# Mixer C's six projection tiles moved from the first stage to the low-priority dense work beside mixer A's recurrence

## The chip, the cores and the metric

The kernel runs on one core of one Trainium2 chip. The metric is the device time of one execution in microseconds (us); lower is better. Beside the time of each run there is one profiled execution, with every engine's instructions: PE (TensorE, matmuls; PEld its weight loads), DVE (VectorE), ACT (ScalarE), POOL (GpSimd) and SP, whose queue issues most of the DMAs.

## The reference

One layer of a hybrid decoder trunk, in float32, for 2048 prompt tokens and 8 x 8 sample tokens (2112 tokens in all) of width 1024. One combined projection `x @ w_in` feeds three mixers; their outputs are projected, normalised, and pass a gated feed-forward block. Cut to what matters here:

```python
proj = x @ w_in
(qa, ka, va, za, ba, aa, xb, gb, qc, kc, vc, zc, lc) = jnp.split(proj, SPLIT_POINTS, axis=-1)

# mixer A: gated DeltaNet, 6 heads of 64, causal conv on q, k, v, chunks of 64 tokens
qkv, dconv_new = causal_dwconv(jnp.concatenate([qa, ka, va], axis=-1), st_dconv, conv_a_w)
qa, ka, va = jnp.split(jax.nn.silu(qkv), [QK_A, 2 * QK_A], axis=-1)
...
oa, delta_new = gated_delta_chunked(l2norm(qa) * DK_A ** -0.5, l2norm(ka), va, beta, g, st_delta)
oa = head_rms_norm(oa, norm_a_w) * jax.nn.silu(za)

# mixer B: RG-LRU of width 256 on xb, gated by gelu(gb)
...
# mixer C: gated linear attention, 6 heads (dk=32, dv=64); q and k are 192 wide, v and z 384
qc = qc * DK_C ** -0.5
logf = jax.nn.log_sigmoid((lc @ gla_w2 + gla_b2)) / GLA_TAU
oc, gla_new = gla_chunked(qc, kc, vc, logf, st_gla)
oc = head_rms_norm(oc, norm_c_w) * jax.nn.silu(zc)

heads = jnp.concatenate([oa, ob, oc], axis=-1)
x = layer_norm(ALPHA * x + heads @ w_out, ln1_g, ln1_b)
f, fconv_new = conv_ffn(x, st_fconv, ffn_w_up, ffn_conv_w, ffn_conv_b, ffn_w_down)
x = layer_norm(ALPHA * x + f, ln2_g, ln2_b)
```

## The kernel before

A float32 product is made from three single-pass matmuls over operands that are split into two rounded parts, high and low: `wh*xh`, `wl*xh` and `wh*xl`. A rounded part `h` is an ACT copy, the rest `lo` is a subtraction on DVE or POOL. Projections are cut into tiles of 128 columns of `w_in` and blocks of tokens; a tile on a block takes 8 x 3 = 24 matmuls into one PSUM buffer.

The program has four parts, one after the other, and only the ends of neighbours overlap.

**Stage 1** (`phase1`, until about 527 us). Twenty tiles of `w_in` (`NT1`), five blocks of tokens (`NBS`: four of 448, one of 320). All of x stays in SBUF as `xh` and `xl`. The matmuls are L320 into `pm`, in five PSUM buffers. After the first two, tiles go in pairs, and the pairs mix a tile with much work behind it and one with little: `small` (decays) with `cq`, `xb 0` (mixer B) with `ck`, `xb 1` with `cqk`, and so on. Six of the twenty are mixer C's: `cq`, `ck`, `cqk` (the last 64 columns of both), and three of `vc`. What follows a tile (`post`) runs on ACT and DVE: for mixer C's tiles one ACT copy and a store to memory; for the others a convolution, activations, scans. `split_w` makes a tile's weight parts (ACT L346, DVE L347).

**Window A** (`window_a`, about 527 to 1017 us). Mixer A's recurrence (`deltanet`) in batches of four chunks: decays and scores (`pcl`, `pa`, `pk`), an inverse by substitution on DVE (L895, L897; `Tm`, `tmp`), and a chain over 32 chunks (`cw`: two products per chunk, with ACT copies between them, then outputs `po`). The last chunks are `cw70` to `cw73`; `cws`, `ss` and `po2048` belong to the sample tokens. Beside it runs the dense work of `gates`: the gate tiles `za` and `zc`, 16 units (2 groups x 8 blocks of tokens, `ZBS`: seven of 256, one of 320), each of 3 steps t = 0, 1, 2, a step being a tile on a block: 24 matmuls into `zp` (L1121 to L1123), an ACT copy to `zo` (L1127), and a store (L1128). `zpU_t` is step t of unit U. There is one PSUM buffer for `zp`. The unit's x comes as four quarters `zx` (L1087), each split by ACT (`xh`, L1088) and POOL (`xl`, L1089). There are four buffers of each part, so that a quarter of the next unit can come only once step t = 2 of this unit has used the same quarter.

**Window C** (`window_c`, to about 1498 us). Mixer C, with operands filled per head (`K`, `Q`), scores `s`, a chain `cs`, and beside it the output projection (`pm` from L320 again, weights `wos`, `woh`, `wol`). It reads `s_cq`, `s_ck`, `s_cv` and `s_zc` back from memory; `s8` are the scores of the sample tokens (group 8, which comes first), `s0_0` those of head 0 in group 0, `pv80` the first transpose of the sample values.

**Stage 3** (`phase3`): the feed-forward block, to the end.

In window A and window C a scheduler sets the order of each engine's instructions when the program is built, by priorities and its own estimate of times; once built, each engine's queue runs in that order. `need` and `ahead` in `window_a` say only how far the dense work has been written out when the recurrence reaches a place.

## Time and profile before

| | us |
|---|---|
| median of 3 runs | 3035.48 |
| lowest, highest | 3034.46, 3045.13 |
| span of the profiled execution | 3039.2 |

The span is from the first to the last instruction of the profiled execution; it is 3.7 us (0.12%) above the median of the runs, and the profile gives no other time of that execution. In the profile's rows a line is followed by its engine, operation, output<-input and shapes; "x64" is a count. SPq rows are DMA issues. PEclk is the TensorE clock that the chip granted, 1.00 being full speed. A recorded matmul lasts longer than its share of the engine, because the next one overlaps it: its cost in a stream is the distance between two starts.

### The profile page before, as it was taken

What the parts mean: (1) busy time and instruction counts of PE and PEld (TensorE: products, weight loads), DVE (VectorE), ACT (ScalarE), POOL (GpSimd) and SP (SyncE); (2) the same over time, 40 slices, a digit from 0 to 9 for tenths busy, and PEclk for the clock granted to TensorE, in tenths of its full rate; (3) what the DMA queues carried; (4) which work ended last, traced back from release to release, by engine and by line L of the source; (5) the groups of instructions that cost most, each with busy time, mean ns of one, the idle gap of its engine ahead of it and who ended that gap; (6) DMA issues with size and microseconds to landing.
All of it is one profiled execution on the core that took longest, in us unless ns stands there. A gap on an engine that the chain in (4) does not pass through costs nothing.

```text
span 3039.2 us, 44833 instructions
## 1 busy us (share of the span) xinstructions
PE 2895.7 (95%) x17755; PEld 2496.9 (82%) x17755; DVE 1597.9 (53%) x2654; ACT 1231.6 (41%) x2591; POOL 843.4 (28%) x892
## 2 busy tenths in 40 slices
PE   8999999789889899998899999999999999999998
PEld 7888789678778677776678888888889999999997
DVE  4564442587665688978533333333366444334446
ACT  4474443446665567756332222222232222222223
POOL 0000001734523545434322222222232222222224
PEclk9999999689898679999999999999999999999999
DMA  6221112433433333322431111111124111111111
GB/s 197 83 74 70 56 61 100 137 106 107 123 99 91 81 120 109 111 82 87 160 123 50 49 42 63 42 56 42 49 104 152 42 47 51 49 42 42 48 43 62
DMA packets 182106, 247.20 MB, mean 81 GB/s; under 512 B 37986, under 2 KB 147640, under 8 KB 181832
## 3 DMA queue, kind: packets, MB, share of 16 engines
q1 hardware_dynamic: 179768, 237.02, 24.2%
q0 software_dynamic: 1984, 7.12, 0.6%
q8 instruction: 140, 2.29, 0.3%
q14 instruction: 70, 0.57, 0.1%
q10 hardware_dynamic: 144, 0.20, 0.0%
HBM read 183.94 MB, written 60.08 MB: 80 GB/s over the span
## 4 chain that ended last, share of the span: by engine, by line
PE 79%; DVE 10%; ACT 4%; issue 3%; DMA 2%; POOL 2%; SPq 0%; POOLq 0%; ACTq 0%; DVEq 0%
PE pm L320 20%; PE pd L320 15%; PE pug L320 15%; PE puv L320 15%; PE s L1364 2%; PE zp L1121 1%; DVE Tm L897 1%; DVE y L1779 1%; DVE tmp L895 1%; DVE K L1337 1%; PE zp L1122 1%; ACT WU L920 1%; PE zp L1123 1%; PE pd L1861 1%; DMA fxl<-s_x1T 1%
## 5 line engine op out<-in xcount | busy, mean ns | idle before, releaser
L1715 DVE SCALAR_TENSOR_TENSOR act<-G,cols,act 128x1024 f32<-128x1024 f32 (+1 forms) x132 | 123.6, 950 | 493.5 <-ACT act L1713 491.1
L1868 DVE TENSOR_TENSOR y<-y,pd 128x512 f32<-128x512 f32 x322 | 220.9, 687 | 203.3 <-PE pd L320 196.8
L1606 POOL TENSOR_TENSOR wl_d<-ws_d,wh_d 128x1024 fp32r<-128x1024 f32 x44 | 106.2, 2415 | 571.3 <-ACT wh_d L1605 547.3
L320 PE MATMUL pd<-wh_d,hh 128*128 128x512 f32 x704 | 215.8, 391 | 4.4 <-DVE y L1868 2.6
L320 PE MATMUL pd<-wh_d,hl 128*128 128x512 f32 x704 | 215.4, 391 | 0.0
L320 PE MATMUL pd<-wl_d,hh 128*128 128x512 f32 x704 | 214.9, 390 | 0.0
L1695 ACT COPY G<-pug 128x512 f32<-128x512 f32 (+2 forms) x110 | 55.2, 503 | 386.3 <-PE pug L320 386.3
L320 PE MATMUL pug<-fxh,wh_g 128*128 128x512 f32 (+2 forms) x880 | 197.0, 352 | 5.3 <-ACT fxh L1658 2.7
L320 PE MATMUL pug<-fxl,wh_g 128*128 128x512 f32 (+2 forms) x880 | 196.6, 352 | 2.5 <-POOL fxl L1659 1.5
L320 PE MATMUL puv<-fxh,wl_v 128*128 128x512 f32 (+2 forms) x880 | 197.1, 353 | 1.1 <-POOL wl_v L1606 1.1
L320 PE MATMUL puv<-fxh,wh_v 128*128 128x512 f32 (+2 forms) x880 | 197.1, 353 | 0.0
L320 PE MATMUL puv<-fxl,wh_v 128*128 128x512 f32 (+2 forms) x880 | 196.9, 352 | 0.0
L320 PE MATMUL pug<-fxh,wl_g 128*128 128x512 f32 (+2 forms) x880 | 196.2, 352 | 0.3 <-POOL wl_g L1606 0.3
L320 PE MATMUL pm<-xh,wh 128*128 128x448 f32 (+1 forms) x800 | 181.9, 360 | 8.3 <-ACT xh L370 6.7
L1605 ACT CAST wh_d<-ws_d 128x1024 fp32r<-128x1024 f32 x44 | 45.7, 1039 | 339.1 <-PE pd L1861 174.9
L320 PE MATMUL pm<-xh,wl 128*128 128x448 f32 (+1 forms) x800 | 181.7, 359 | 0.0
L320 PE MATMUL pm<-xl,wh 128*128 128x448 f32 (+1 forms) x800 | 180.0, 358 | 0.1
L1757 DVE TENSOR_TENSOR hl<-act,hh 128x512 fp32r<-128x512 f32 (+2 forms) x110 | 124.1, 1128 | 99.5 <-ACT hh L1749 99.5
L320 PEld LDWEIGHTS pug<-fxh,wh_g 128*128 128x128 f32 x880 | 156.2, 188 | 21.7 <-ACT fxh L1658 4.3
L320 PEld LDWEIGHTS pug<-fxl,wh_g 128*128 128x128 f32 x880 | 155.7, 188 | 16.9 <-POOL fxl L1659 2.0
L320 PEld LDWEIGHTS puv<-fxh,wl_v 128*128 128x128 f32 x880 | 156.1, 189 | 15.3 <-POOL wl_v L1606 1.3
L320 PEld LDWEIGHTS pm<-xh,wh 128*128 128x128 f32 x800 | 144.6, 188 | 28.9 <-issue 10.1
(731 smaller groups left out, 6371.0 us busy)
## 6 DMA issues: line engine op xcount, KB each, us to landing
ws_d<-in_w_dn SPq DMA_DIRECT2D x44, 512.0 KB
ws_g<-in_w_up SPq DMA_DIRECT2D x43, 512.0 KB
ws_v<-in_w_up SPq DMA_DIRECT2D x43, 512.0 KB
zx<-in_xT SPq DMA_DIRECT2D x56, 256.0 KB
ws<-in_w_in SPq DMA_DIRECT2D x19, 512.0 KB
x<-in_x SPq DMA_DIRECT2D x16, 512.0 KB
s_x<-x SPq DMA_DIRECT2D x16, 512.0 KB
s_x1T<-xt SPq DMA_DIRECT2D x16, 512.0 KB
```

The source lines that it names most:

```text
L320: nc.tensor.matmul(ps, w[k], x[k], start=first and i == 0, stop=last and i == 3 * n - 1)
L895: nc.vector.tensor_tensor(t, Y[:, j + 1:, j:j + 1].to_broadcast([128, k, j + 1]), Tm[:, j:j + 1, :j + 1].to_broadcast([128, k, j + 1]), op ...
L897: nc.vector.tensor_tensor(Tm[:, j + 1:, :j + 1], Tm[:, j + 1:, :j + 1], t, op=OP.subtract)
L920: nc.scalar.copy(o[:, h, :, :, jh * 32:(jh + 1) * 32], Ut[r, :, :3 * mt].rearrange("p i (a c) -> p a c i", a=3)[:, :, g.c0:g.c0 + m])
L1121: nc.tensor.matmul(ps, wh[:, k], xl, start=k == 0, stop=False)
L1364: nc.tensor.matmul(ps[64:, c], K[:, i], Q[:, i], start=True, stop=True)
L1605: nc.scalar.copy(h, t)
L1606: nc.gpsimd.tensor_tensor(lo, t, h.bitcast(F32), op=OP.subtract)
L1695: nc.scalar.copy(G[:, 2 + o:2 + o + m], p[:, :m])
L1715: nc.vector.scalar_tensor_tensor(dst(act), src(i), taps[i], dst(act), op0=OP.mult, op1=OP.add)
L1757: nc.vector.tensor_tensor(dst, act[:, c], hh[:, c].bitcast(F32), op=OP.subtract)
L1868: nc.vector.tensor_tensor(y, y, ps, op=OP.add)
```

## The change

Mixer C's six tiles leave stage 1 and join the dense work of `gates`, which now has four groups of three tiles (`za`; `cq`, `ck`, `cqk`; `vc`; `zc`) and 32 units. Stage 1 has 14 tiles in other pairs. Stage 1 stores its two parts of x to memory (`s_xh`, `s_xl`), and a unit loads both parts (eight loads) instead of splitting x again. The dense matmuls and the loads of x within them get a priority of -10^5. `split_w` subtracts on POOL instead of DVE; `zo` has two buffers. Comments and documentation strings are gone, so line numbers move by a few.

```diff
     one("gb", 0), one("gb", 1)
-    tiles.append(("small", 0, small)), tiles.append(("cq", 0, o["qc"] + r))
-    one("xb", 0), tiles.append(("ck", 0, o["kc"] + r))
-    one("xb", 1), tiles.append(cqk)
-    one("ka", 0), one("vc", 0)
+    tiles.append(("small", 0, small)), one("xb", 0)
+    one("xb", 1), one("ka", 0)
     one("ka", 1), one("ka", 2)
     one("qa", 0), one("qa", 1)
     one("qa", 2), one("va", 0)
-    one("va", 1), one("vc", 1)
-    one("va", 2), one("vc", 2)
-    for n in ("za", "zc"):
+    one("va", 1), one("va", 2)
+    for n in ("za", "c", "vc", "zc"):
+        if n == "c":
+            tiles.extend([("cq", 0, o["qc"] + r), ("ck", 0, o["kc"] + r), cqk])
+            continue
...
-NT1 = len(W_TILES) - 6
+NT1 = len(W_TILES) - 12
...
+    for n in ("xh", "xl"):
+        E.s[n] = E.dpool.tile([DM, TT], F32, name="s_" + n)
...
             nc.scalar.copy(wh, W[ct])
-            nc.vector.tensor_tensor(wl, W[ct], wh.bitcast(F32), op=OP.subtract)
+            nc.gpsimd.tensor_tensor(wl, W[ct], wh.bitcast(F32), op=OP.subtract)
...
+            if ct in (3, 4):
+                nm, part = (("xh", xh), ("xl", xl))[ct - 3]
+                nc.sync.dma_start(s[nm].rearrange("(k p) t -> p k t", p=128)[:, :, t0:t0 + n], part[nb].bitcast(F32))
...
-    op = ctx.enter_context(tc.tile_pool(name="z4", bufs=1))
+    op = ctx.enter_context(tc.tile_pool(name="z4", bufs=2))
...
-    units = [(nm, nb) for nm in ("za", "zc") for nb in range(len(ZBS))]
+    units = [(gr, nb) for gr in range(4) for nb in range(len(ZBS))]
...
-        h, lo = (xp.tile([128, 640], F32R, tag=x, name=f"{x}{u}_{j}")[:, :2 * n].rearrange("p (k t) -> p k t", k=2)
-                 for x in ("xh", "xl"))
-        split(h, lo, xTv[:, 2 * j:2 * j + 2, t0:t0 + n], f"zx{u}_{j}")
-        X[u, j] = h, lo
+        both = []
+        for x in ("xh", "xl"):
+            t = xp.tile([128, 640], F32R, tag=x, name=f"{x}{u}_{j}")[:, :2 * n].rearrange("p (k t) -> p k t", k=2)
+            nc.sync.dma_start(t.bitcast(F32), xv[x][:, 2 * j:2 * j + 2, t0:t0 + n])
+            both.append(t)
+        X[u, j] = both
...
             for t in range(3):
-                ps = pm.tile([128, 320], F32, tag="zp", name=f"zp{u}_{t}")[:, :n]
-                wh, wl = W[i0 + t]
-                for k in range(KD):
...
+                with tc.high_priority(-10 ** 5):
+                    ps = pm.tile([128, 320], F32, tag="zp", name=f"zp{u}_{t}")[:, :n]
+                    wh, wl = W[3 * gr + t]
+                    for k in range(KD):
+                        xh, xl = (a[:, k % 2] for a in X[u, k // 2])
+                        nc.tensor.matmul(ps, wh[:, k], xl, start=k == 0, stop=False)
+                        nc.tensor.matmul(ps, wl[:, k], xh, start=False, stop=False)
+                        nc.tensor.matmul(ps, wh[:, k], xh, start=False, stop=k == KD - 1)
+                        if t == 2 and k % 2 == 1:
+                            load_x(u + 1, k // 2)
...
-                nc.scalar.copy(o, ps)
-                nc.sync.dma_start(s[nm][t * 128:(t + 1) * 128, t0:t0 + n], o)
+                kind, tt, _ = W_TILES[NT1 + 3 * gr + t]
+                c = slice(t0, t0 + n)
+                if kind == "cqk":
+                    nc.scalar.activation(o[:64], ps[:64], AF.Copy, scale=32 ** -0.5)
+                    nc.scalar.copy(o[64:], ps[64:])
+                    nc.sync.dma_start(s["cq"][128:192, c], o[:64])
+                    nc.sync.dma_start(s["ck"][128:192, c], o[64:])
+                else:
+                    nc.scalar.activation(o, ps, AF.Copy, scale=32 ** -0.5 if kind == "cq" else 1.0)
+                    nc.sync.dma_start(s["cv" if kind == "vc" else kind][tt * 128:(tt + 1) * 128, c], o)
...
         def ahead(i):
-            while count[0] < (4, 20, 36, 52)[i]:
+            while count[0] < (8, 40, 72, 104)[i]:
```

The built program shows where the scheduler puts the dense work. On PE, where window A ends: before, the last dense step `zp15_2` stands between chunks of mixer A's chain (`cw71`, of the last four) and the sample's outputs.

```order
L1122 MATMUL zp15_2_8942<-xh15_3_8877,zl5_7259 128x320
L1123 MATMUL zp15_2_8942<-xh15_3_8877,zh5_7258 128x320
L965 MATMUL cw71_9560<-X1_4422,KD1_4424 64x64 x6
L1016 MATMUL po2048_9363<-R3_4419,X8_4429 64x64
L977 MATMUL po1792_9536<-R2_4418,X1_4422 64x64 x12
```

With the change, on PE at the same place: `zp15_2` stands behind all of the chain, then come the first scores of window C (`s8`, `s0_0`), and then `zp16_0` to `zp31_2`, 1152 matmuls in one block, before `pv80`, the next instruction of window C.

```order
L1114 MATMUL zp15_2_7123<-xh15_3_7038,zl5_5538 128x320
L1115 MATMUL zp15_2_7123<-xh15_3_7038,zh5_5537 128x320
L1364 MATMUL s8_0_10571<-Q2_s0_10402,K2_s0_10401 64x64
...
L1364 MATMUL s30_0_10986<-Q3_0_10394,K3_0_10393 64x64 x4
L1113 MATMUL zp16_0_7179<-xl16_0_7132,zh6_7075 128x256
...
L1115 MATMUL zp31_2_9627<-xh31_3_9564,zh11_7999 128x320
L1385 MATMUL pv80_10543<-c_ident_10465,v_8_10485 64x128
```

So units 0 to 13 stand beside the recurrence, where 0 to 15 stood before, and the rest in a block of their own. On SP's queue within that block, around unit 17 (`s_cv<-zo` are stores of steps, `xl`, `xh` the loads of the next unit's quarters 0 to 3):

```order
L1128 DMA s_cv_68<-zo16_1_7232 128x256
L1095 DMA xl17_0_7244<-s_xl_76 128x2x256
L1095 DMA xh17_0_7242<-s_xh_75 128x2x256
L1095 DMA xh17_1_7252<-s_xh_75 128x2x256
L1095 DMA xl17_1_7254<-s_xl_76 128x2x256
L1095 DMA xh17_2_7262<-s_xh_75 128x2x256
L1095 DMA xl17_2_7264<-s_xl_76 128x2x256
L1128 DMA s_cv_68<-zo16_2_7276 128x256
L1095 DMA xh17_3_7272<-s_xh_75 128x2x256
L1095 DMA xl17_3_7274<-s_xl_76 128x2x256
L1128 DMA s_cv_68<-zo17_0_7304 128x256
```

Before, the same queue had four loads of a unit, on their way to ACT and POOL:

```order
L1087 DMA zx14_0_8735<-in_xT 128x2x256
...
L1087 DMA zx14_1_8747<-in_xT 128x2x256
...
L1128 DMA s_zc_69<-zo13_0_8695 128x256
L1128 DMA s_zc_69<-zo13_1_8723 128x256
L1087 DMA zx14_2_8759<-in_xT 128x2x256
```

Eight loads and three stores a unit stand there now; the load of the last quarter stands behind the store of the unit before.

More of the change, by code (lines that the diff above doesn't have):

```diff
@@ L580, in post_act @@
             if fn is None:
-                if name == "cq":
-                    nc.scalar.activation(o, ps, AF.Copy, scale=32 ** -0.5)
-                elif name == "cqk":
-                    nc.scalar.activation(o[:64], ps[:64], AF.Copy, scale=32 ** -0.5)
-                    nc.scalar.copy(o[64:], ps[64:])
-                else:
-                    nc.scalar.copy(o, ps)
+                nc.scalar.copy(o, ps)
             else:
@@ L657, in post @@
                 r = slice(t * 128, (t + 1) * 128)
-                c = slice(t0, t0 + n)
-                if kind == "cqk":
-                    nc.sync.dma_start(s["cq"][128:192, c], o[:64])
-                    nc.sync.dma_start(s["ck"][128:192, c], o[64:])
-                else:
-                    nc.sync.dma_start(s[{"gb": "gg", "vc": "cv"}.get(kind, kind)][r, c], o)
+                nc.sync.dma_start(s["gg"][r, t0:t0 + n], o)
         def norms():
@@ L1076, in gates @@
     sp = ctx.enter_context(tc.tile_pool(name="z3", bufs=2))
-    op = ctx.enter_context(tc.tile_pool(name="z4", bufs=1))
+    op = ctx.enter_context(tc.tile_pool(name="z4", bufs=2))
     pm = ctx.enter_context(tc.tile_pool(name="zm", bufs=1, space=PSUM))
-    xTv = E.d["xT"].rearrange("(k p) t -> p k t", p=128)
-    units = [(nm, nb) for nm in ("za", "zc") for nb in range(len(ZBS))]
+    xv = {n: s[n].rearrange("(k p) t -> p k t", p=128) for n in ("xh", "xl")}
+    units = [(gr, nb) for gr in range(4) for nb in range(len(ZBS))]
     W, X = {}, {}
-    def split(h, lo, src, name):
-        k, n = src.shape[1:]
-        st = sp.tile([128, 640], F32, tag="zs", name=name)[:, :k * n].rearrange("p (k t) -> p k t", k=k)
-        nc.sync.dma_start(st, src)
-        nc.scalar.copy(h, st)
-        nc.gpsimd.tensor_tensor(lo, st, h.bitcast(F32), op=OP.subtract)
     def load_w(i):
@@ L1094, in load_w @@
         for j in (0, 4):
-            split(h[:, j:j + 4], lo[:, j:j + 4], E.d["w_in"][NT1 + i][:, j:j + 4], f"zw{i}_{j}")
+            st = sp.tile([128, 4, 128], F32, tag="zs", name=f"zw{i}_{j}")
+            nc.sync.dma_start(st, E.d["w_in"][NT1 + i][:, j:j + 4])
+            nc.scalar.copy(h[:, j:j + 4], st)
+            nc.gpsimd.tensor_tensor(lo[:, j:j + 4], st, h[:, j:j + 4].bitcast(F32), op=OP.subtract)
         W[i] = h, lo
@@ L1111, in steps @@
         load_w(1), load_w(2)
-        for u, (nm, nb) in enumerate(units):
+        for u, (gr, nb) in enumerate(units):
             t0, n = ZBS[nb]
-            last = u == len(ZBS) - 1
-            i0 = 0 if nm == "za" else 3
+            last = nb == len(ZBS) - 1 and gr < 3
             for t in range(3):
-                ps = pm.tile([128, 320], F32, tag="zp", name=f"zp{u}_{t}")[:, :n]
-                wh, wl = W[i0 + t]
-                for k in range(KD):
-                    xh, xl = (a[:, k % 2] for a in X[u, k // 2])
-                    nc.tensor.matmul(ps, wh[:, k], xl, start=k == 0, stop=False)
-                    nc.tensor.matmul(ps, wl[:, k], xh, start=False, stop=False)
-                    nc.tensor.matmul(ps, wh[:, k], xh, start=False, stop=k == KD - 1)
-                    if t == 2 and k % 2 == 1:
-                        load_x(u + 1, k // 2)
-                o = op.tile([128, 320], F32, tag="zo", name=f"zo{u}_{t}")[:, :n]
-                nc.scalar.copy(o, ps)
-                nc.sync.dma_start(s[nm][t * 128:(t + 1) * 128, t0:t0 + n], o)
+                with tc.high_priority(-10 ** 5):
[8 more added lines that the diff above has]
+                            load_x(u + 1, k // 2)
+                o = op.tile([128, 320], F32, tag="zo", name=f"zo{u}_{t}")[:, :n]
+                kind, tt, _ = W_TILES[NT1 + 3 * gr + t]
[8 more added lines that the diff above has]
+                    nc.sync.dma_start(s["cv" if kind == "vc" else kind][tt * 128:(tt + 1) * 128, c], o)
@@ L1129, in steps @@
                 if last:
-                    load_w(3 + t)
+                    load_w(3 * gr + 3 + t)
                 yield
-            E.z_done.add((nm, nb))
+            E.z_done.add((gr, nb))
     return steps()
@@ L1151, in need @@
             for nb, (a, w) in enumerate(ZBS):
-                while a < t0 + n and t0 < a + w and ("za", nb) not in E.z_done:
+                while a < t0 + n and t0 < a + w and (0, nb) not in E.z_done:
                     count[0] += 1
```

## Prediction

> **What bounds the kernel now.** I read the page's head first, then the table of stretches, then the rows of the two kinds of projection matmul.
>
> ```profile
> span 3039.2 us, 44833 instructions
> PE 2895.7 (95%) x17755; PEld 2496.9 (82%) x17755; DVE 1597.9 (53%) x2654; ACT 1231.6 (41%) x2591; POOL 843.4 (28%) x892
> ```
>
> PE is the bound on average, but the change moves work between two stages, so the stages decide. The table has, for each stretch, its length, the busy time of PE, PEld, DVE, ACT and POOL, the granted clock, the DMA share and GB/s:
>
> ```profile
> core 0: us, PE busy (x) PEld busy (x) DVE busy (x) ACT busy (x) POOL busy (x), PEclk, DMA share, GB/s
> 60.00:160.00 100.00, 100.00 (x479) 85.25 (x478) 54.16 (x80) 51.27 (x83) 0.10 (x1) 1.00 0.24 75
> 160.00:240.00 80.00, 80.00 (x394) 70.74 (x393) 46.38 (x89) 56.76 (x92) 3.05 (x9) 1.00 0.26 81
> 240.00:444.00 204.00, 204.00 (x966) 164.05 (x965) 92.46 (x154) 84.43 (x189) 6.56 (x25) 1.00 0.17 62
> 444.00:527.00 83.00, 83.00 (x434) 77.20 (x433) 28.58 (x50) 30.82 (x63) 9.65 (x19) 1.00 0.28 87
> 527.00:640.00 113.00, 83.86 (x662) 77.64 (x661) 69.98 (x130) 53.75 (x105) 71.21 (x80) 0.71 0.45 129
> 640.00:900.00 260.00, 234.45 (x2739) 209.80 (x2739) 184.36 (x340) 158.28 (x322) 100.68 (x114) 0.91 0.38 109
> 900.00:960.00 60.00, 50.96 (x479) 43.58 (x478) 40.53 (x110) 42.52 (x149) 25.21 (x44) 0.86 0.34 97
> 960.00:1017.00 57.00, 57.00 (x584) 50.17 (x582) 17.62 (x22) 21.89 (x59) 25.47 (x21) 0.89 0.24 69
> 1017.00:1102.00 85.00, 70.59 (x492) 52.48 (x491) 74.74 (x166) 59.47 (x176) 40.74 (x74) 0.58 0.46 138
> ```
>
> Stage 1 (to 527) is PE from end to end at full clock: what leaves PE there leaves the time. Window A (527 to 1017) has idle PE and a lower clock, so on paper it has room. The order of the built program says that the room is not used: units 0 to 13 of the dense work stand beside the recurrence, no more than before, and units 14 to 31 behind it, 16 to 31 in one block, with window C's next work behind that. PE runs in order. So I cost the change as: a shorter stage 1, a recurrence with slightly less in it, and a new stretch, the dense tail, that nothing on PE fills.
>
> **Stage 1.** Cost of its matmuls, from starts (64 of 448 columns between the first two rows, 16 of 320 between the others):
>
> ```profile
> 454.52 1.79 PE L320 MATMUL pm<-xh,wh 128*128 128x448 f32 x8
> 467.53 1.79 PE L320 MATMUL pm<-xl,wh 128*128 128x448 f32 x8
> 469.16 1.34 PE L320 MATMUL pm<-xh,wh 128*128 128x320 f32 x8
> 471.51 1.33 PE L320 MATMUL pm<-xl,wh 128*128 128x320 f32 x8
> ```
>
> (467.53 - 454.52) / 64 = 0.203 us, and (471.51 - 469.16) / 16 = 0.147 us. A tile is 24 x (4 x 0.203 + 0.147) = 23.0 us, six tiles 138. With them goes the light half of the pairs that hid mixer B. The rows of what goes with a tile of C (its copy on a block, and its two weight parts):
>
> ```profile
> 524.08 0.53 ACT L587 COPY ovc<-pm 128x448 f32<-128x448 f32 x1 [1.49 <-PE pm L320]
> L346 ACT CAST wh<-ws 128x1024 fp32r<-128x1024 f32 x19 | 19.9, 1047 | 30.0 <-PE pm L320 22.6 <-DMA ws<-in_w_in 7.3
> L347 DVE TENSOR_TENSOR wl<-ws,wh 128x1024 fp32r<-128x1024 f32 x19 | 23.2, 1223 | 26.1 <-ACT wh L346 25.9
> ```
>
> Between 60 and 240 us ACT is busy 108 of 180 us and DVE 101. Three tiles of C leave there: 69 us of PE, 15 x 0.53 + 3 x 1.05 = 11 of ACT, 4 of DVE. `ka 0` is drawn in: 23 of PE and, by the mix of 240 to 444 us (ACT 84, DVE 92 in 204), about 10 of each. That leaves 107 of ACT and 107 of DVE beside 134 of PE: 80%, with waits between them. I take 12 us of PE waiting, between 0 and 24. The stores of x, 17.3 MB, take 54 us of DMA at the rate below, in stretches where the DMA share is 0.24 to 0.26: nothing, covered. So is `split_w` on POOL, which is all but idle there; the low part is needed only after eight matmuls, 1.6 us. A load behind such a store on SP's queue (`gg`) comes some 6 us late and is used three steps on. **Stage 1: -126 (-138 to -114).**
>
> **The recurrence.** The order takes 150 matmuls out of it: a quarter of `zp13_2` and units 14 and 15. A dense matmul of 256 columns at full clock and at the low one, from starts 21 and 6 matmuls apart:
>
> ```profile
> 843.11 0.28 PE L1123 MATMUL zp<-xh,zh 128*128 128x256 f32 x1
> 845.62 0.28 PE L1123 MATMUL zp<-xh,zh 128*128 128x256 f32 x1
> 556.02 0.41 PE L1123 MATMUL zp<-xh,zh 128*128 128x256 f32 x1
> 557.30 0.41 PE L1123 MATMUL zp<-xh,zh 128*128 128x256 f32 x1
> ```
>
> 0.1195 and 0.213 us. 78 x 0.1195 + 72 x 0.147 = 20 us, where PE is busy 57 of 57 us (960 to 1017). The splits of x go too:
>
> ```profile
> L1089 POOL TENSOR_TENSOR xl<-zx,xh 128x512 fp32r<-128x512 f32 x56 | 74.0, 1335 | 114.8 <-ACT xh L1088 95.6 <-issue 14.8 <-DMA kv<-s_v 1.7
> L1088 ACT CAST xh<-zx 128x512 fp32r<-128x512 f32 x56 | 34.1, 617 | 34.2 <-DMA zx<-in_xT 24.1 <-PE zp L1123 8.1 <-POOL xl L1089 0.9
> ```
>
> About 85 us of POOL and 39 of ACT with the wider ones, of which POOL counts only at the start (71 of 113 us busy, 527 to 640): 5 us, my choice. Against it stand four more loads a unit, 15 MB, at a DMA share of 0.38: nothing, covered. SP's queue still waits there for PE's buffers, as it waited for POOL's. **Recurrence: -25 (-45 to -5).**
>
> **The dense tail.** How fast does a unit go alone? Rows for it: a load of 256 KB from its issue to the ACT cast that waited for it, twice; the spacing of issues on SP; the DMA's rate at a 72% share, and in a mix of small packets; the last matmul of a step and the copy of its PSUM buffer.
>
> ```profile
> 954.05 0.38 SPq L1087 DMA_DIRECT2D zx<-in_xT  x1
> 957.07 0.62 ACT L1088 CAST xh<-zx 128x512 fp32r<-128x512 f32 x1 [2.94 <-DMA zx<-in_xT]
> 549.37 0.55 SPq L1087 DMA_DIRECT2D zw<-in_w_in  x1
> 552.46 0.62 ACT L1088 CAST zh<-zw 128x512 fp32r<-128x512 f32 x1 [3.04 <-DMA zw<-in_w_in]
> 532.75 0.43 SPq L309 DMA_DIRECT2D c_ident<-in_consts  x1
> 534.17 0.43 SPq L309 DMA_DIRECT2D c_bj<-in_consts  x1
> q1 hardware_dynamic: 9328, 13.94, 72.2%
> q1 hardware_dynamic: 63282, 46.00, 36.2%
> 966.50 0.28 PE L1123 MATMUL zp<-xh,zh 128*128 128x256 f32 x1
> 966.86 0.37 ACT L1127 COPY zo<-zp 128x256 f32<-128x256 f32 x1 [3.12 <-PE zp L1123]
> ```
>
> Load: 3.0 to 3.1 us. Issues: 1.42 / 3 = 0.47 us apart. Rate: 13.94 MB in 60 us at 72.2% is 322 GB/s of a full DMA (the first 60 us); 46.00 MB in 440 us at 36.2% is 289 (560 to 1000). 256 KB at 322 is 0.81 us. Turnaround of the one PSUM buffer: from the last start to the copy's end 0.73, to the next start about 0.8, so 0.68 beyond the 0.12 of the matmul itself.
>
> A quarter of x is free for loading only when step t = 2 of the unit before has used it. From that step's start: quarter 0 is used at 0.9, its two loads are issued at 1.0 and 1.5, the others follow; the first lands at 4.0, and the eight, with the store that stands among them, come at 0.8 a load: quarters whole at 4.8, 6.4, 8.0 and 10.0. Step 0 is paced by them and ends at 10.7; + 0.7, step 1 (24 x 0.1195 = 2.9), + 0.7: the next step 2 starts at 15.0. So **15 us a unit, of which PE computes 8.6**. A unit of 320 columns by the same sum: 17.7.
>
> The tail: 14 units of 256 (16 to 22, 24 to 30) 210, three of 320 (15, 23, 31) 53, unit 14 between the sample's last products 10: 273. To this: (1) `zp16_0` stands behind window C's first scores on PE, and `zo16` behind their fills on ACT; they need `s_cq`, which unit 15 ends. Beside the recurrence, that took 34 us:
>
> ```profile
> 906.94 3.30 DMA q<-s_cq
> 940.98 0.72 PE s L1364 x5
> ```
>
> Alone I take 22, and 3 for the weights of unit 24 on the same queue: 25 (10 to 34). (2) The clock: with PE waiting in every quarter it will look more like 527 to 640 (granted 0.71, PE 84 of 113 us busy) than like stage 1. All at the low rate, steps 1 and 2 add about 3 us a unit, 51 in all; I take half, 24 (0 to 51). **Tail: +322 (+249, with loads at 0.7 us, to +360).**
>
> [...]
>
> **Window C** starts behind the tail with what it had at 1017 before (`s8`, `s0_0`), but the chain's and the sample's leftovers, three weight loads and some fills are done. Of the 85 us to its first projection (DVE busy 75) I take off 15 (0 to 30). Stage 3 is untouched.
>
> **Sum:** 3039 - 126 - 25 + 322 - 15 = 3195 for a profiled execution; less the 3.7 us by which the profile's span is over the median, 3191. I say **3190 us**.
>
> **Rivals.**
> 1. *The recurrence was paced by the splits* (not slower). Place: 527 to 1017, 490 us; PE in order stood behind x, and x behind ACT and POOL. The floor is DVE: 70 + 184 + 41 + 18 = 313 us busy, so at most 177 saved instead of 25: 3190 - 152 = 3038, no change. It decides from about 165. Against it: the inverse and the chain, which do not change, wait on each other, and as many dense steps stand among them. 4%.
> 2. *The loads are hidden, the tail runs at PE's pace*: 3 x (2.87 + 0.68) = 10.7 us a unit of 256, 12.7 of 320, so 10 + 150 + 38 + 10 = 208 instead of 322: 3076. Still slower. For it: a unit needs 2.5 MB, 7.7 us of DMA, less than 10.7. Against it: the buffers come free only in step 2. 8%.
> 3. *Tail and stage 1 at their bad ends*: cold clock, a gate of 34, PE waiting 24 in stage 1 and the recurrence slowed by loads: 3190 + 38 + 12 + 20 = 3260. 20%.
> 4. *The forecast*, 3110 to 3235 with its terms nearer their middles: 68%.
>
> The range takes the forecast and most of 3: 3095 to 3265. What this kernel's measurement can tell from no change is about 0.5% (15 us). Faster by more: 2%; within: 3%; slower: 95%.
>
> **What would show it.** In the profile after: `pm` in stage 1 ends near 400 us; the chain `cw73` near 865; then 300 us in which only `zp` is on PE, with SP's `xh` and `xl` loads waiting for PE and `zp` waiting for DMA, DVE all but idle, the clock under 1; `pm` of window C near 1260. A unit's distance (start of `zp17_0` to `zp18_0`) says 15 or not. I am wrong if units come every 11 us, if stage 1 does not shrink by 110, or if the recurrence is over long before 850.

## The result, and the profile after

The changed kernel takes 3281.5 us (median of 4 runs) beside 3035.0 us of the kernel before on the same chip: ratio 1.0815, interval 1.0794 to 1.0836. The forecast had the sign and the new stretch on PE, but stood at 3190 with an end at 3265: 91 us too low, and 16 us past that end. The profiled execution has a span of 3285.3 us, 246 us more than before.

The head of the page of the changed kernel:

```profile
span 3285.3 us, 45957 instructions
PE 2998.2 (91%) x18187; PEld 2579.2 (79%) x18187; DVE 1555.6 (47%) x2635; ACT 1213.6 (37%) x2565; POOL 802.4 (24%) x853
```

Its table of stretches, with the columns of the prediction's (length; busy time of PE, PEld, DVE, ACT, POOL; granted clock; DMA share; GB/s):

```profile
20.00:100.00 80.00, 57.93 (x245) 49.81 (x245) 15.11 (x16) 21.02 (x29) 5.17 (x3) 0.85 0.89 316
100.00:140.00 40.00, 40.00 (x185) 32.77 (x185) 21.56 (x31) 22.50 (x35) 0.10 (x1) 1.00 0.18 59
140.00:280.00 140.00, 119.08 (x510) 95.09 (x509) 97.68 (x162) 100.50 (x161) 14.46 (x18) 0.91 0.20 64
280.00:458.00 178.00, 173.47 (x820) 141.16 (x819) 90.28 (x146) 80.92 (x179) 25.93 (x38) 0.98 0.21 68
458.00:921.00 463.00, 403.20 (x4262) 362.06 (x4261) 260.86 (x557) 218.26 (x479) 110.02 (x152) 0.83 0.47 139
921.00:985.00 64.00, 42.88 (x245) 34.33 (x243) 27.11 (x76) 31.36 (x105) 18.67 (x41) 0.76 0.73 220
985.00:1274.00 289.00, 216.42 (x1149) 191.10 (x1148) 0.00 (x0) 23.86 (x59) 7.69 (x6) 0.76 0.45 140
1274.00:1355.00 81.00, 63.27 (x475) 50.72 (x475) 65.14 (x116) 50.13 (x147) 49.35 (x62) 0.66 0.36 106
```

Two rows stand out. From 985 to 1274 DVE does nothing: this is the dense tail that was forecast, only longer. From 20 to 100 us the DMA is full (0.89) and PE idles 22 of 80 us; the kernel before had there:

```profile
20.00:100.00 80.00, 80.00 (x389) 69.49 (x388) 32.43 (x37) 36.02 (x56) 0.47 (x1) 1.00 0.42 135
140.00:240.00 100.00, 100.00 (x495) 88.75 (x494) 58.96 (x108) 69.44 (x112) 3.15 (x10) 1.00 0.25 78
```

To compare runs by stage I take four marks in each trace: the start of stage 1's last `pm<-xh,wh`, of the chain's last `cw<-X,KD`, of the last `zo`, of window C's last `pm<-woh,mh`. In the changed kernel the groups of `pm` and of `cw` give them so ("first to last start" stands after the durations):

```profile
L322 PE MATMUL pm<-xh,wh x560: 304/366/1255, 6.6 to 455.9; 128*128 128x448 f32 x150, 128*128 128x320 f32 x37
L959 PE MATMUL cw<-X,KD x384: 222/222/369, 609.4 to 920.4; 128*64 128x64 f32 x192
```

| us | before | after | difference | forecast |
|---|---|---|---|---|
| stage 1, to the mark | 524.9 | 455.9 | -69 | -126 |
| recurrence | 491.3 | 464.5 | -27 | -25 |
| tail (last `cw` to last `zo`) | none | 354.0 | +354 | +322 |
| window C | 480.1 | 473.4 | -7 | -15 |
| rest of the span | 1542.9 | 1537.5 | -5 | 0 |

Of the 90 us, 57 belong to stage 1 and 32 to the tail.

**Why PE starves at the start.** SP's queue from 12 us on, in the changed kernel (start, us, what is issued):

```profile
11.96 0.89 SPq L371 DMA_DIRECT2D xs<-in_xT  x2
14.13 0.37 SPq L689 DMA_DIRECT2D s_xh<-xh  x1
14.59 0.53 SPq L371 DMA_DIRECT2D xs<-in_xT  x1
15.18 1.26 SPq L689 DMA_DIRECT2D s_xl<-xl  x1
17.64 2.37 SPq L342 DMA_DIRECT2D ws<-in_w_in  x1
20.18 6.74 SPq L371 DMA_DIRECT2D xs<-in_xT  x3
32.87 0.37 SPq L689 DMA_DIRECT2D s_xh<-xh  x1
```

The code writes the stores of x's parts (L689) behind the fourth and fifth tile, that is behind the first two, which take 46 us by the forecast's 23 us a tile; the prediction took their place from there. The scheduler orders the queues of stage 1 too, not only those of windows A and C: in the built program the stores stand as soon as their block is split, two of 1.8 MB among the loads (`xs`, 448 KB each) of the next block of x, which the first two tiles wait for. The groups of the changed kernel between 20 and 100 us show the chain from the load to PE (busy, mean ns, then idle time ahead and what ended it):

```profile
L322 PE MATMUL pm<-xh,wh 128*128 128x448 f32 (+1 forms) x80 | 26.0, 399 | 21.9 <-ACT xh L372 20.9 <-ACT wh L348 0.8
L372 ACT CAST xh<-xs 128x896 fp32r<-128x896 f32 (+1 forms) x14 | 12.0, 880 | 48.6 <-DMA xs<-in_xT 48.6
```

**One unit of the tail.** The timeline from step 1 of unit 20 (1061.24) over its step 2 (1067.26) and unit 21's step 0 (1071.03) to its step 1 (1081.36): the PE rows that waited, and the first and the last issue of unit 21's eight loads.

```profile
1061.24 0.58 PE L1113 MATMUL zp<-xl,zh 128*128 128x256 f32 x1 [0.52 <-ACT zo L1127]
1067.26 0.39 PE L1113 MATMUL zp<-xl,zh 128*128 128x256 f32 x1 [0.52 <-ACT zo L1127]
1068.03 0.37 SPq L1095 DMA_DIRECT2D xl<-s_xl  x1
...
1071.03 0.35 PE L1113 MATMUL zp<-xl,zh 128*128 128x256 f32 x1 [0.64 <-DMA xl<-s_xl]
1071.67 0.38 PE L1114 MATMUL zp<-xh,zl 128*128 128x256 f32 x1 [0.29 <-DMA xh<-s_xh]
1072.04 0.82 SPq L1095 DMA_DIRECT2D xl<-s_xl  x1
1074.51 0.58 PE L1113 MATMUL zp<-xl,zh 128*128 128x256 f32 x1 [1.98 <-DMA xl<-s_xl]
1079.18 0.58 PE L1113 MATMUL zp<-xl,zh 128*128 128x256 f32 x1 [1.42 <-DMA xl<-s_xl]
1081.36 0.58 PE L1113 MATMUL zp<-xl,zh 128*128 128x256 f32 x1 [0.52 <-ACT zo L1127]
```

Five stretches of the same time, in the columns of the table above:

```profile
1061.00:1067.00 6.00, 5.49 (x24) 5.20 (x24) 0.00 (x0) 0.37 (x2) 0.00 (x0) 0.50 0.06 22
1069.00:1077.00 8.00, 5.09 (x28) 4.27 (x27) 0.00 (x0) 0.38 (x1) 0.00 (x0) 0.81 0.90 276
1077.00:1082.00 5.00, 3.05 (x13) 2.47 (x13) 0.00 (x0) 0.38 (x1) 0.00 (x0) 0.50 0.02 7
1077.00:1078.00 1.00, 0.76 (x4) 0.47 (x3) 0.00 (x0) 0.00 (x0) 0.00 (x0) 0.50 0.06 22
1078.00:1079.00 1.00, 0.00 (x0) 0.00 (x0) 0.00 (x0) 0.00 (x0) 0.00 (x0) 0.50 0.04 14
```

The eight loads overlap and fill the DMA for about 8 us (0.90); the last is used 11.9 us after step 2 began. The DMA is not quiet before that: from 1077.0 to 1078.7 its share is that of one of its 16 engines (0.06), which is still moving packets, and PE goes on 0.5 us after the last one. So late a last quarter is not the rule: of the tail's other units only one shows it (PE goes on at 1172.77). PE waits 0.6, 0.3, 2.0 and 1.4 us for the loads. In the wait of 2.0 the granted clock falls to 0.50, and it is back at 1.00 some 10 us later; at the low clock a step takes up to 6.0 us (1061.24 to 1067.26) instead of 3.7 (e3_same_x, below).

### The profile page after: what moved, and what is told of

Its sections match the earlier page's. It is cut to its first block, busy times and chain, and to the rows that moved or that the text cites. A ratio compares the mean times of both kernels' runs of the same rounds, so it can differ in the third digit from the quotient of the medians.

```text
span 3285.3 us, 45957 instructions
## 1 busy us (share of the span) xinstructions
PE 2998.2 (91%) x18187; PEld 2579.2 (79%) x18187; DVE 1555.6 (47%) x2635; ACT 1213.6 (37%) x2565; POOL 802.4 (24%) x853
## 4 chain that ended last, share of the span: by engine, by line
PE 72%; DMA 8%; DVE 8%; ACT 6%; issue 3%; SPq 2%; POOL 1%; ACTq 0%; DVEq 0%; POOLq 0%
PE pug L322 14%; PE pd L322 14%; PE puv L322 14%; PE pm L322 12%; DMA xl<-s_xl 4%; PE zp L1113 3%; PE zp L1114 2%; PE zp L1115 2%; DMA xs<-in_xT 1%; PE s L1364 1%; DVE y L1779 1%; ACT WU L914 1%; PE pw L938 1%; PE cw L956 1%; DVE K L1337 1%
## 5 line engine op out<-in xcount | busy, mean ns | idle before, releaser
L1113 PE MATMUL zp<-xl,zh 128*128 128x256 f32 (+1 forms) x768 | 275.9, 359 | 86.1 <-DMA xl<-s_xl 60.6
L1113 PEld LDWEIGHTS zp<-xl,zh 128*128 128x128 f32 x768 | 177.3, 231 | 118.5 <-DMA xl<-s_xl 63.7
L1114 PE MATMUL zp<-xh,zl 128*128 128x256 f32 (+1 forms) x768 | 255.1, 332 | 8.6 <-DMA xh<-s_xh 8.6
L1115 PE MATMUL zp<-xh,zh 128*128 128x256 f32 (+1 forms) x768 | 252.0, 328 | 0.0
L1114 PEld LDWEIGHTS zp<-xh,zl 128*128 128x128 f32 x768 | 180.4, 235 | 13.9 <-DMA xh<-s_xh 11.0
L1115 PEld LDWEIGHTS zp<-xh,zh 128*128 128x128 f32 x768 | 179.0, 233 | 1.5 <-issue 1.2
L322 PE MATMUL pm<-xh,wh 128*128 128x448 f32 (+1 forms) x560 | 141.5, 386 | 42.4 <-ACT xh L372 27.5
L1757 DVE TENSOR_TENSOR hl<-act,hh 128x512 fp32r<-128x512 f32 (+2 forms) x110 | 124.2, 1129 | 99.5 <-ACT hh L1749 99.5
```

The lines of the kernel that those rows point to most:

```text
L322: nc.tensor.matmul(ps, w[k], x[k], start=first and i == 0, stop=last and i == 3 * n - 1)
L1113: nc.tensor.matmul(ps, wh[:, k], xl, start=k == 0, stop=False)
L1114: nc.tensor.matmul(ps, wl[:, k], xh, start=False, stop=False)
L1115: nc.tensor.matmul(ps, wh[:, k], xh, start=False, stop=k == KD - 1)
L1757: nc.vector.tensor_tensor(dst, act[:, c], hh[:, c].bitcast(F32), op=OP.subtract)
```

## Experiments

Marks of all runs (us from the span's start; "rec." and "tail" are the lengths between marks; the median is over the runs of that kernel):

| run | stage 1 | rec. | tail | window C ends | span | median | ratio to before on the same chip, interval |
|---|---|---|---|---|---|---|---|
| before | 524.9 | 491.3 | - | 1496.3 | 3039.2 | 3035.0 | 1 |
| after | 455.9 | 464.5 | 354.0 | 1747.8 | 3285.3 | 3281.5 | 1.0815, 1.0794 to 1.0836 |
| e1_late_stores | 422.5 | 453.7 | 360.9 | 1706.9 | 3246.1 | 3236.8 | 1.0672, 1.0643 to 1.0702 |
| e4_no_low_priority | 456.5 | 533.4 | 186.1 | 1648.2 | 3190.1 | 3185.2 | 1.0492, 1.0462 to 1.0522 |
| e5_parts_alone | 555.6 | 478.3 | - | 1509.7 | 3051.2 | 3057.3 | 1.0079, 1.0058 to 1.0100 |
| e6_split_again | 422.3 | 477.9 | 353.2 | 1729.9 | 3269.0 | 3267.1 | 1.0770, 1.0751 to 1.0789 |
| e3_same_x | 456.5 | 469.7 | 164.2 | 1564.9 | 3101.3 | 3103.6 | 1.0225, 1.0210 to 1.0240 |
| e8_half_loads | 455.4 | 458.4 | 215.6 | 1593.1 | 3131.4 | 3126.3 | 1.0301, 1.0280 to 1.0322 |
| e7_light_pairs | 412.2 | 477.3 | 324.3 | 1686.4 | 3225.8 | 3221.9 | 1.0608, 1.0589 to 1.0626 |
| e9_before_late_parts | 524.2 | 482.3 | - | 1482.3 | 3026.9 | 3034.0 | 0.9991, 0.9977 to 1.0004 |
| e11_merged_loads | 458.1 | 473.6 | 304.8 | 1706.4 | 3247.4 | 3252.7 | 1.0718, 1.0703 to 1.0734 |
| e12_all_fixes | 413.5 | 554.6 | 140.6 | 1580.3 | 3126.6 | 3110.7 | 1.0249, 1.0226 to 1.0272 |
| e14_merged_long_runs | 414.5 | 536.6 | 138.2 | 1561.9 | 3104.1 | 3102.8 | 1.0220, 1.0203 to 1.0237 |
| e15_split_on_dve | 413.5 | 547.2 | 135.3 | 1564.8 | 3100.3 | 3107.3 | 1.0241, 1.0224 to 1.0258 |

### The stores of x

**e1_late_stores.** A store waits for the weights of a later tile: a small write of them to the same place goes ahead of it.

```diff
-            if ct in (3, 4):
-                nm, part = (("xh", xh), ("xl", xl))[ct - 3]
-                nc.sync.dma_start(... part[nb] ...)
+            if nb == 2 and ct >= 4:
+                j = (ct - 4) // 2
+                nm, part = (("xh", xh), ("xl", xl))[ct % 2]
+                a, w = NBS[j]
+                nc.sync.dma_start(s[nm][0:128, a:a + 1], wh[:, 0, 0:1].bitcast(F32))
+                nc.sync.dma_start(... part[j] ...)
```

> The changed kernel, but each of the ten stores of x's parts is held back until a later tile's weights are there (one from about 100 us on, every second or third tile step), so that they no longer stand among the loads of x on SP's queue. Theory S (the stores starve PE in the first 100 us): PE's waits for ACT's xh between 20 and 100 us (20.9 us by cause, 22 us of PE idle) go down to the 7 us that they were before the change, stage 1 ends near 430 us instead of 458, and the time falls by 20 to 30 us to about 3255. Rival C (stage 1's lost gain is all the missing cover of mixer C's tiles): stage 1 stays within 8 us of 458, 3275 to 3285. The tail is not touched under either: a unit of 256 stays at 18 to 19 us.

Measured 3236.8 us, 45 less than the changed kernel. Stage 1 ends 33 us earlier. The same stretch as above, in this run:

```profile
20.00:100.00 80.00, 80.00 (x389) 69.78 (x388) 30.86 (x38) 39.34 (x59) 5.26 (x3) 1.00 0.40 130
...
140.00:280.00 140.00, 120.41 (x515) 94.21 (x514) 90.91 (x153) 86.25 (x147) 12.52 (x18) 0.91 0.32 103
```

PE is back at 80 of 80 us with the same 389 matmuls as before the change. Theory S holds, but its price was higher than the 20 to 30 us that I had given. By the marks the recurrence is 11 us shorter too and the tail 7 longer; what the stores did there I did not look into.

**e5_parts_alone.** The kernel before, with `s_xh` and `s_xl` stored as in the change and loaded in `load_x`; nothing else of the change.

```diff
-        split(h, lo, xTv[:, 2 * j:2 * j + 2, t0:t0 + n], f"zx{u}_{j}")
+            nc.sync.dma_start(t.bitcast(F32), xv[x][:, 2 * j:2 * j + 2, t0:t0 + n])
```

> The kernel before with one part of the change alone: stage 1 stores x's two parts and the gates load them (eight loads a unit) instead of splitting x again; mixer C's tiles stay in stage 1. Theory S (stores beside the loads of x starve PE at the start): stage 1 ends 20 to 30 us later than 527, the recurrence is within 10 us of its 490 us: 3055 to 3065. Rival 1 of the prediction (the recurrence was paced by the splits of x): the recurrence is shorter by 40 us or more, 3020 or less. Rival H (with more tiles the stores hide): 3025 to 3040.

Measured 3057.3 us. Stage 1 is 31 us longer with mixer C's tiles in it, as it was without them: the early stores alone cost that. The recurrence is 13 us shorter, a little more than the 10 of theory S, which is what the removed splits were worth with the eight loads in their place. Rival 1 of the prediction, in which the splits paced the recurrence, needed 40 or more and falls.

```profile
20.00:100.00 80.00, 59.49 (x248) 51.97 (x247) 16.91 (x17) 21.11 (x29) 0.47 (x1) 0.85 0.90 323
```

**e9_before_late_parts.** The kernel of e5_parts_alone with the late stores of e1_late_stores.

> The kernel before with x's parts stored late (as in e1_late_stores) and loaded in the dense work; mixer C's tiles stay in stage 1. In e5_parts_alone stage 1 grew by 30 us and the recurrence shrank by 12 to 14. Theory S: without the early stores stage 1 ends at 527 to 530 again and the recurrence keeps its gain: 3020 to 3030, faster than both kernels. Rival (17.3 MB of stores cost PE a share wherever they stand, through ws and gg loads behind them on SP's queue): stage 1 ends at 535 or later, 3035 to 3045.

Stage 1 is as before (524.2), the recurrence keeps 9 us. Median 3034.0 us, ratio 0.9991 (0.9977 to 1.0004): not told from the kernel before. Stage 1 lies where theory S put it, but its 3020 to 3030 us did not come: 9 us (0.3%) are within what the runs scatter (3022.5 to 3045.5), so a gain is not shown.

**e6_split_again.** Mixer C's tiles stay in the dense work; nothing is stored, and the dense work splits x as before, with one `zo` buffer.

```diff
-            nc.sync.dma_start(t.bitcast(F32), xv[x][:, 2 * j:2 * j + 2, t0:t0 + n])
+        nc.sync.dma_start(st, xTv[:, 2 * j:2 * j + 2, t0:t0 + n])
+        nc.scalar.copy(both[0], st)
+        nc.gpsimd.tensor_tensor(both[1], st, both[0].bitcast(F32), op=OP.subtract)
```

> The changed kernel with the other half of the change undone: no stores of x, the dense work loads x itself (four loads of 256 KB a unit) and splits it on ACT and POOL as the kernel before did, with one zo buffer as there (there is no room for two). Mixer C's tiles stay in the dense work. Theory S with loads as the pace of the tail: stage 1 ends near 430 us; a unit of the tail takes 0.9 us + a load of 3.0 + ACT 0.6 + four subtractions on POOL of 1.34 each = 9.9 us to the last quarter, about as long as the eight loads' 10 to 12: 16 to 18.5 us a unit; 3225 to 3255. Rival (the splits are worse in the tail than the loads): a unit over 20 us, 3270 or more.

Measured 3267.1 us: 15 less than the changed kernel, but 12 over the range I gave. Stage 1 ends at 422.3 without any stores, as in e1_late_stores with late ones. The recurrence is 13 us longer than after. The tail is as long as with stored parts (353 beside 354): half the bytes, but each quarter then goes through ACT (0.62) and POOL (1.27), and PE waits 54 us for POOL's parts between 960 and 1253. So storing x's parts bought 13 us of recurrence for 33 of stage 1.

### What is left in stage 1

**e7_light_pairs.** e1_late_stores with other pairs.

```diff
-    tiles.append(("small", 0, small)), one("xb", 0)
+    tiles.append(("small", 0, small)), one("va", 0)
+    one("xb", 0), one("va", 1)
     one("xb", 1), one("ka", 0)
 ...
-    one("qa", 2), one("va", 0)
-    one("va", 1), one("va", 2)
+    one("qa", 2), one("va", 2)
```

> The kernel of e1_late_stores with two pairs of stage 1 changed: small stands beside va 0 and xb 0 beside va 1, and small and xb 0 no longer beside each other; the other pairs move up. Theory C (what is left of stage 1's missing gain, about 23 us, is PE waiting for ACT and DVE where small, xb 0 and xb 1 come close together): PE's idle time between 100 and 280 us (24 us in e1_late_stores) falls by half or more and stage 1 ends 10 to 25 us earlier, at 400 to 414; the time falls by as much, 3212 to 3227. Rival (ACT and DVE have the same sum to do, wherever it stands): stage 1 within 6 us of 424, 3230 to 3245.

Measured 3221.9 us, 15 less. Stage 1 ends 10 us earlier; the rest is not its own, for 1.7 more units stand ahead of the chain's last product (the recurrence is 24 us longer, the tail 37 shorter). Between 100 and 280 us:

```profile
100.00:280.00 180.00, 165.84 (x757) 138.07 (x756) 120.59 (x203) 135.37 (x222) 23.29 (x35) 0.96 0.39 130
```

PE's idle time there is 14.2 us, in e1_late_stores 24.7; 4.5 us of idle time stand between 280 and 414 instead, where e1_late_stores has none. So a part of the loss is one of cover, and spreading mixer B's tiles over `va` recovers it: theory C, just short of its half and at the lower end of its 10 to 25 us. What holds the rest is not shown.

### The tail

**e3_same_x.** x is loaded for the first unit only.

```diff
-        if u >= len(units):
-            return
-        t0, n = ZBS[units[u][1]]
+        if u:
+            X[u, j] = X[0, j]
+            return
+        t0, n = ZBS[7]
```

> The changed kernel, but x is loaded for the first unit only and every later unit computes with that x (its loads are left out). In the built order 18 units instead of 13 then stand ahead of the chain's last product, 14 behind it. Theory L (the loads pace the tail, and the low clock follows from the waiting): a unit of 256 in the tail takes 3 x (2.87 + 0.7 to 0.8) = 10.7 to 11 us, the granted clock there is 0.95 to 1.00; the recurrence grows by 4 to 5 units of 8.6, the tail falls from 353 to 170 to 190 us: 3125 to 3160. Rival T (the tail is slow for another reason, the one PSUM buffer with its copy, or a clock that falls when the other engines have no work): a unit stays over 14 us, 3190 or more.

**e8_half_loads.** Only `xh` is loaded, and used for both parts.

```diff
-        for x in ("xh", "xl"):
+        for x in ("xh",):
 ...
-            both.append(t)
+            both += [t, t]
```

> The changed kernel, but a unit loads only the high part of x and uses it in the place of the low part too: four loads of 256 KB a unit instead of eight. In the built order two to three more units stand ahead of the chain's last product. Theory L: from the start of step 2 the last quarter comes free at 2.9, its load lands 3.1 to 4.6 us later, step 0 ends at 7 to 8.2, then 0.7 + 2.9 to 5.1 (full or low clock) + 0.7: 11.5 to 14.5 us a unit of 256 instead of 18.6; with two to three units less in the tail 3150 to 3200. Rival T (not the loads): 17 us or more a unit, 3240 or more.

Measured 3103.6 and 3126.3 us. The recurrence and the stretch behind it, of e3_same_x and then of e8_half_loads, beside clocks of 0.83 and 0.76 in the changed kernel:

```profile
458.00:926.00 468.00, 416.55 (x4620) 380.01 (x4619) 282.04 (x613) 247.77 (x582) 128.80 (x191) 0.93 0.30 87
985.00:1090.00 105.00, 90.64 (x668) 84.86 (x666) 0.00 (x0) 14.02 (x33) 7.64 (x6) 1.00 0.14 47
```

```profile
458.00:914.00 456.00, 407.43 (x4482) 369.96 (x4482) 282.47 (x609) 241.08 (x564) 127.16 (x188) 0.90 0.41 119
985.00:1129.00 144.00, 113.69 (x799) 103.28 (x797) 0.00 (x0) 16.36 (x39) 7.69 (x6) 0.99 0.39 123
```

A unit of 256 takes 10.97 us without loads (from one copy of `zp` to the next 3.66, three of them), 12.2 with half of them, 18.4 with all (six units from 995.73 to 1107.87 and six from 1146.66 to 1255.05). Theory L holds; rival T falls: the one PSUM buffer costs about the 0.7 us a step that were forecast, and the clock is all but whole where PE waits less. In its stretch PE of e8_half_loads still stands idle for 30.3 of 144 us, and the clock keeps 0.99: the longest first step of a unit of 256, unit 24's, takes 6.36 us from copy to copy (1027.50 to 1033.86), and the two behind it 3.65 and 3.66, as in e3_same_x. Its time is 24 us under its range: 16.7 units instead of 13.9 start ahead of the chain's last product, and the recurrence is 6 us shorter all the same.

e3_same_x came out 22 us under its range, because of the recurrence: 4.4 more units start in it (18.3 instead of 13.9), and it is 5 us longer, where I had counted 8.6 for each. The first row above goes with that: a clock of 0.93 there, 0.83 in the changed kernel.

**e11_merged_loads.** After, with both parts of x in one array `s_xx` and one load for a quarter.

```diff
-            nc.sync.dma_start(t.bitcast(F32), xv[x][:, 2 * j:2 * j + 2, t0:t0 + n])
+        nc.sync.dma_start(t.bitcast(F32), s["xx"][:, 4 * j:4 * j + 4, t0:t0 + n])
```

> The changed kernel with both parts of x in one array (rows of the high and the low part alternate) and one load of 512 KB for a quarter instead of two of 256 KB: four issues a unit, the same bytes, the same runs of 1 KB. In the built order one unit more stands ahead of the chain's last product. Theory B (the tail waits for bytes: 2.1 MB a unit at the rate that the DMA had there, and the latency ahead of them): a unit of 256 stays at 17.5 to 19 us, 3260 to 3280. Rival I (it waits for SP's issues, 0.47 us each and late ones behind them): a unit falls to 13 to 15.5 us, 3195 to 3240.

Measured 3252.7 us; a unit 17.2 (five from 987.28 to 1073.22), clock 0.77 from 985 to 1236. The issues are not the pace: rival I falls. The time is 7 us under theory B's range, since 1.7 units more than in the changed kernel start in the recurrence and a unit is 1.2 us shorter.

**e14_merged_long_runs** stands on e12_all_fixes (below): a quarter is one run of 4 KB on each partition.

```diff
-        nc.sync.dma_start(t.bitcast(F32), s["xx"][:, 4 * j:4 * j + 4, t0:t0 + n])
+        nc.sync.dma_start(t.bitcast(F32), s["xx"][:, 2 * KD * t0 + 4 * j * n:2 * KD * t0 + 4 * (j + 1) * n] ...)
```

> The kernel of e12_all_fixes with x's two parts stored so that a quarter of a unit (both parts) is one run of 4 KB on each partition, loaded by one DMA of 512 KB. The same bytes as in e12_all_fixes, in four issues and runs four times as long. Theory B: 8 units behind the chain stay near 18 us each, the time within 15 us of e12_all_fixes. Rival R (long runs load faster): a unit of 256 falls to 12 to 15 us, 30 to 50 us less than e12_all_fixes.

Measured 3102.8 us beside 3110.7 of e12_all_fixes. A unit takes 17.0 us (six from 968.86 to 1071.08), in e12_all_fixes 18.7 (five from 996.29 to 1089.80). Two stretches of one unit:

```profile
1003.00:1010.00 7.00, 3.69 (x25) 3.02 (x24) 0.00 (x0) 0.38 (x1) 0.00 (x0) 0.90 0.98 353
1010.00:1019.00 9.00, 8.25 (x36) 7.66 (x36) 0.00 (x0) 0.53 (x2) 0.00 (x0) 0.51 0.06 23
```

The DMA moves more (353 GB/s at 0.98) and is done a little earlier, but PE still waits for 2 MB that cannot be asked for before step 2, and then computes for 9 us at half clock. Rival R falls.

**e15_split_on_dve.** As e12_all_fixes, but no stores: four loads of x a unit, split on ACT and DVE (the edit against e6_split_again).

```diff
-        nc.gpsimd.tensor_tensor(both[1], st, both[0].bitcast(F32), op=OP.subtract)
+        nc.vector.tensor_tensor(both[1], st, both[0].bitcast(F32), op=OP.subtract)
```

> Mixer C's tiles in the dense work, but with no stores of x at all: a unit loads x itself (four loads of 256 KB, half the bytes) and splits it on ACT and DVE, which has nothing to do behind the recurrence; one zo buffer; pairs, priority and the early writing out of the dense work as in e12_all_fixes. In the built order 23 units stand ahead of the chain's last product, 9 behind it. Theory B (the tail waits for bytes, and its clock falls with the waits): the last quarter lands as in e8_half_loads, plus ACT 0.62 and DVE some 0.6 us behind it, and a unit of 256 takes 13 to 15 us instead of 18.6; the recurrence pays DVE's splits (under 1 us a quarter, 92 quarters) with up to 13 us, as e6_split_again against the changed kernel: 3080 to 3110. Rival (the two staging buffers and the chain load, ACT, DVE pace it as ACT and POOL did in e6_split_again): 17 us a unit, 3115 to 3140. Not faster than the kernel before under either.

Measured 3107.3 us. Theory B by its unit: one of 256 takes 13.1 us (four from 1024.97 to 1077.27), and the clock is whole:

```profile
1024.00:1078.00 54.00, 40.74 (x298) 36.61 (x297) 12.06 (x18) 15.22 (x30) 0.00 (x0) 1.00 0.36 110
```

Yet the time is that of e12_all_fixes. The recurrence is 7 us shorter, but with one unit less in it, and the tail has one unit more. Its first units are not quick either: copies of `zp` end units at 973.51, 991.83, 1011.60 and 1024.97, so 18.3, 19.8 and 13.4 us apart, beside window C's first loads (a DMA share of 0.91 from 990 to 1010).

### Where the dense work stands

**e4_no_low_priority.** After, without the priority of the dense matmuls.

```diff
-                with tc.high_priority(-10 ** 5):
+                with ExitStack():
```

> The changed kernel without the priority of -10^5 on the dense matmuls and their loads; nothing else. In the built order 22 units instead of 13 then stand ahead of the chain's last product, and 9 to 10 behind it instead of 18. Theory P (a unit beside the recurrence costs PE's 8.6 us or a little more, one behind it 18 to 19): the recurrence grows by 8 x 9 to 8 x 13 = 70 to 105 us, the tail shrinks by 8 x 18.5 = 148: 45 to 80 us less, 3200 to 3237. Rival Q (the chain stands behind each dense step on PE and each step costs the chain its whole length): the recurrence grows by 150 or more and the time does not change, 3270 to 3300.

Measured 3185.2 us, 96 less than the changed kernel: better than theory P's range. The recurrence grows by 69 us for 8.1 more units, 8.5 us each and so PE's own, and the tail shrinks by 168, 21 us a unit.

**e12_all_fixes.** e7_light_pairs without the priority, and written out earlier.

```diff
-            while count[0] < (8, 40, 72, 104)[i]:
+            while count[0] < (40, 104, 104, 104)[i]:
```

> The kernel of e7_light_pairs (late stores, other pairs in stage 1) without the low priority, and with the dense work written out earlier (40 steps ahead of the first batch's blocks, all of it ahead of the second's). In the built order 24 units stand ahead of the chain's last product, 8 behind it. Theory P (a unit beside the recurrence costs PE's 8.6 us, one behind it 18.6): against e7_light_pairs' 3222 nine to ten units less behind the chain, 10 us each, 3120 to 3130; if the recurrence has idle PE left that they fill, down to 3095. Rival (the recurrence is full: each further unit beside it costs more than 12 us): 3150 or more. Neither is faster than the kernel before.

Measured 3110.7 us: inside theory P, between its two cases. A unit more in the recurrence costs 9.0 us (77 us for 8.6 units, beside e7_light_pairs). Still 75 us over the kernel before. Its sum against before: stage 1 -111, recurrence +63, tail +141, window C -8, rest +3: +87 by the profiled executions (3126.6 was the longest of its six runs).

## Why the prediction was right or wrong

**Stage 1: wrong, by 57 of 126 us; two terms failed.** The first is "the stores of x ... nothing, covered". They cost 33 us (e1_late_stores, e6_split_again; 31 in e5_parts_alone). Their size was not far off: 17.3 MB are 49 us of a full DMA at the rate of the stretch above (316 GB/s at 0.89), for the 54 forecast. The place was wrong. I put them where the code has them, "in stretches where the DMA share is 0.24 to 0.26"; the built order of SP's queue has the first of them between the loads of the second block of x (14 us in the trace), where the kernel before shows a DMA share of 0.42 over 20 to 100 us, and where the loads of x are what PE waits for. I had read the built order for PE, and for SP in the tail, but not for SP in stage 1.

The second is the cover: "PE waiting, 12 us, between 0 and 24". From 138 us of matmuls, 102 were saved with late stores: 36 lost for 12. 25 of them are idle PE between 100 and 280 us, just past the end of that range; the rest goes with a lower clock (0.91 to 0.96 there), for which the term had nothing. That the tiles stood together is a part of it (e7_light_pairs): I averaged ACT and DVE over 180 us (80% busy), while the waits come where mixer B's tiles meet. The sum also left out the loads of ACT's function tables, 22 in stage 1 before and 33 after, 14 us more of ACT:

```profile
L298 ACT ACT_TABLE_LOAD x22 | 28.2, 1283 | 0.4
L300 ACT ACT_TABLE_LOAD x33 | 42.3, 1283 | 0.6
```

How much of PE's waiting is theirs is not shown; e7_light_pairs has 40 of them and a shorter stage 1, so their number alone does not decide.

**The subtraction on POOL: right.** It takes 2.57 us instead of 1.22, and PE waited 0.6 us for it in all of stage 1.

**Recurrence: right in sum, -27 beside -25, by luck.** The parts were -20 for the matmuls and -5 for the splits; the runs show 13 (e6_split_again beside before) and 13 (e5_parts_alone), so two errors cancel. "Four more loads a unit ... nothing, covered" is not so: with four loads a unit instead of eight (e8_half_loads) 2.8 more units start in the recurrence, and it is 6 us shorter, at a clock of 0.90 instead of 0.83.

**Tail: right in kind, +354 beside +322; here the clock was mis-sized.** Step by step: unit 14's rest and unit 15 took 38 us for 28, which I did not look into; the gate and the weights 25 for 25 (`zp16_0` begins about 984.7, unit 15 ends 959.2); the 16 units 290 for 269. The distance from `zp17_0` to `zp18_0`, which was to decide, is 18.3 us (996.25 to 1014.55), not 15. In those 16 units PE waited for loads of x:

```profile
PE zp L1113 <- DMA xl<-s_xl: 43.9, 36, 2.4
PE zp L1114 <- DMA xh<-s_xh: 6.4, 15, 2.1
```

That is 50 us, less than the 70 in the forecast's units (15.0 instead of 10.7 us for one of 256 columns, 17.7 instead of 12.7 for one of 320). What was too small is "I take half, 24 (0 to 51)" for the clock. Of the tail's 1148 recorded matmuls 457 start at the half clock, 422 of 256 columns 0.213 instead of 0.12 us apart and 35 of 320 columns 0.267 instead of 0.147: 44 us. In the unit shown above, the quarters are whole 4.4, 7.3 and 11.9 us (first, second, last) after the start of step 2, for 4.8, 6.4 and 10.0 in the forecast; the last is late there by the one DMA engine, and that unit took 19.0 us from one step 2 to the next (1067.26 to 1086.26). The low end of the forecast, +249, takes "loads at 0.7 us", which no run shows: 256 KB are 0.85 us at the 307 GB/s of a full DMA in that unit (276 at a share of 0.90), and 0.73 us at the 360 GB/s of e14_merged_long_runs.

What went with the low clock can be read from the traces, and it is not the length of a single wait. In the tail of the changed kernel the granted clock changes only at steps of 3.41 us. It falls 15 times, each time behind a slot of that length in which PE was busy for 25 to 55% (1.21 of 3.41 us in the unit shown, from 1070.55 to 1073.96), and stays low for two or three slots; none of the 30 slots behind which it stayed whole has less than 63%. The longest idle time of PE in one piece within a slot does not part the two: 0.69 to 2.07 us in the 15, up to 1.06 us in the 30. In e8_half_loads the clock stayed whole behind a first step that waits had made 2.7 us longer (6.36 instead of 3.66), and of its steps from 985 to 1129 that are not the first of a unit only one took longer than the others of its width, 5.17 us instead of 3.66 (991.37 to 996.54): 1.5 us more, which is one slot of 3.41 us at the half clock. This is read from the runs' traces; no run was made to test it.

**The gate and window C.** "25 (10 to 34)" came out at 25, from one choice of 22 and one of 3 that no run took apart; window C gave 7 of the 15.

**The rivals.** Rival 2 (the tail at PE's pace) was right about PE's pace (10.97 us for 10.7) and wrong about what paces: only without loads does it come. Rival 3 (the bad ends, 20%) was the nearest, with 3260; it had the cold clock and the lost cover, and lacked the stores.
